# Attention scores of two query tiles made together: second pass on 64 rows, one tile on each row group of TensorE

## The chip, the cores and the metric

The kernel runs on one core of one Trainium2 chip. The metric is the device time of one execution in microseconds (us). Three executions of the kernel before took 3033.25 us in the median, 3031.68 to 3037.04. A profiled execution gives the views that are quoted here; PE is TensorE, PEld its weight loads, DVE is VectorE, ACT ScalarE, POOL GpSimd, SP the engine that issues most transfers.

## What is computed

One layer of a streaming encoder for 2048 prompt frames and 8 x 16 sample frames, all in float32: a mixer (chunked attention beside a convolution module), cross-attention into 256 memory tokens and a gated feed-forward. The change touches the attention of the prompt frames. A query chunk of 64 frames sees its own chunk and the 8 before it, with a bias by relative distance, in 8 heads of 64 channels:

```python
def one_chunk(c):
    start = c * CHUNK
    qc = lax.dynamic_slice_in_dim(q, start, CHUNK, axis=1)
    kc = lax.dynamic_slice_in_dim(k_ext, start, BAND, axis=1)
    ...
    s = jnp.einsum("bqhd,bkhd->bhqk", qc, kc, preferred_element_type=jnp.float32) * scale + bias
    s = jnp.where(valid[None, None, None, :], s, NEG_INF)
    p = jax.nn.softmax(s, axis=-1)
    return jnp.einsum("bhqk,bkhd->bqhd", p.astype(vc.dtype), vc)
```

## The kernel before

The stages follow each other: memory keys and values (to about 150 us), the input projection with the convolution (to 640 us), attention (640 to 925 us), output projection and cross-attention (to about 1600 us), then the feed-forward. Nearly all matmuls take their operands as fp32r, a rounded float32, so each float32 number is split into a high part (`hi`) and a rest (`lo`), and a product is made of two or three matmuls that add up in PSUM.

In the projection, `qk` makes q and k for one pair of heads (`j`) and one group of 384 tokens (`x`), splits them and stores them to DRAM in `self.qs[j]` and `self.ks[j]`, shape [2, 128, 2048]: plane 0 is hi, plane 1 is lo, then 128 channels (two heads of 64), then tokens. The split lands in a buffer `qk`, of which there are two (`qkx` in the last group of tokens), and L717 stores it in one transfer on SP's queue. `qk` runs 24 times for q: 20 times with 384 tokens, 4 times with 128 (tile 15 and the sample frames, whose q is kept on the chip).

In attention, `units` runs over 8 heads and, in each, 16 tiles of 128 queries. `head_load` brings a head in, while the head before is worked on: `q2` holds hi in partitions 0 to 63 and lo in 64 to 127; `k2` holds k's hi twice, in both halves; `kl` holds k's lo twice. `scores` (L850) makes a tile's scores against up to 5 blocks of 128 keys. A matmul with `q2` as weights and `k2` as moving operand contracts over 128 rows and gives (q_hi + q_lo) k_hi; a second one with `kl` adds (q_hi + q_lo) k_lo. With five blocks the keys are cut into 384 and 256 columns, so that each part stays in a PSUM bank; tiles 0 to 3 have 128, 256, 384 and 512 columns. The scores of a tile have a place of 4 KB in PSUM (`"s"`), of which there are two. `softmax_band` adds the bias and finds the maximum on DVE (L793) and takes the exponential on ACT (L795). Four units later `transp` turns the probabilities (L878, transposes of float32 on TensorE, split by ACT at L879 and DVE at L880), six later, at every fourth, `values` multiplies them with v (L891). `sample` does the attention of one sample stream a head between these.

The order on each engine is set by the scheduler of the language, from priorities (the place in the code, raised by `high_priority`), waits and a timeline of its own; `issue_after(ins)` only keeps the block's instructions behind `ins` on its engine. TensorE takes its instructions strictly in that order. Weight loads are instructions of their own, one for each matmul.

Elsewhere TensorE already has matmuls on fewer than 128 rows: L1010 in the output projection (16 rows), L845 in `sample` (16 rows) and, in the feed-forward's `tform`, transposes of 64 rows (L1408).

Of the kernel before, what the change touches and what calls it, by code (L numbers as in the profile page):

```python
# [17 lines left out]
P = 128  # L18
# [5 lines left out]
DH = 64  # L24
# [112 lines left out]
class Build:  # L137
# [309 lines left out]
    def phase_proj(self):  # L447
# [129 lines left out]
        for gi, subs in enumerate(GROUPS):  # L577
# [103 lines left out]
            def qk(which, j, blk, x):  # L681
# [14 lines left out]
                else:  # L696
# [4 lines left out]
                    for i, t in enumerate(sub):  # L701
# [12 lines left out]
                            nc.sync.dma_start(A["new_att_k_sample"][:, PAST - DEC_S:, :], kos[t][:, :])  # L714
                        else:
                            nc.sync.dma_start(A["new_att_k_prompt"][(t - 12) * P:(t - 11) * P, :], kos[t][:, :])
                nc.sync.dma_start(dst[:, :, col:col + npc].rearrange("c p n -> p c n"),  # L717
                                  sp[:, :, :npc].bitcast(F32))

            for j in range(3):  # L720
                for which in (1, 0):
# [61 lines left out]
    def attention(self):  # L783
# [6 lines left out]
        def softmax_band(ps, w, bias, sm):  # L790
            z = self.t(pool, [P, W5], F32, "z", 6)
            nmx = self.t(pool, [P, 1], F32, "nmx", 12)
            nc.vector.tensor_tensor_reduce(out=z[:, :w], in0=ps, in1=bias, scale=-1.0, scalar=3e38,  # L793
                                           op0=ALU.add, op1=ALU.min, accum_out=nmx[:, :])
            nc.scalar.activation(z[:, :w], z[:, :w], AF.Exp, bias=nmx[:, :], scale=-1.0, accum_out=sm)  # L795
            return z
# [50 lines left out]
            nc.vector.tensor_copy(self.attS[:DH, :, ss], po[:DH, :, :DEC_S])  # L847
            nc.vector.tensor_copy(self.attS[DH:, :, ss], po[DH:, :, DEC_S:])

        def scores(hd, t, sm):  # L850
            q2, k2, kl, v2, bt = hd
            j0 = max(0, t - 4)
            nb = t - j0 + 1
            n = nb * P
            tq = slice(t * P, (t + 1) * P)
            ps = self.t(ps_s, [P, 8, P], F32, "s")
            a = 1 if nb == 5 else 0
            for lo, hi in ([(1, 4), (4, 6)] if nb == 5 else [(0, nb)]):
                kk = slice((j0 + lo - a) * P, (j0 + hi - a) * P)
                for x, kx in enumerate((k2, kl)):  # L860
                    nc.tensor.matmul(ps[:, lo:hi, :], q2[:, tq], kx[:, kk], start=x == 0, stop=x == 1)
            return softmax_band(ps[:, a:a + nb, :].rearrange("p a b -> p (a b)"), n, bt[:, W5 - n:], sm)

        def transp(zs, t, quad):
            if t % 4 == 0:
# [50 lines left out]
        for i in range(n + LV + 1):  # L916
            if i < n:
                h, t = units[i]
                if t == 0:
                    fill = sample(h)  # L920
                if t == 6 and h + 1 < H:
                    heads[h + 1] = self.head_tiles(h + 1)
                    self.head_load(h + 1, heads[h + 1], 0, NPT)
                zq[h, t] = scores(heads[h], t, self.sums[:, t, h:h + 1])
            u = i - LT
            if 0 <= u < n:
                h, t = units[u]
# [774 lines left out]
```

## Time and profile before

| | us |
|---|---|
| median of 3 runs | 3033.25 |
| the profiled execution | 3033.59 |
| its span, first to last instruction | 3031.8 |
| TensorE busy in the span | 2949.8 (97%) |
| score matmuls (L861), 448 of them, first and last start | 643.2 to 923.2 |
| granted TensorE clock, mean | 0.987 |

A matmul's row gives its duration from its start to the end of its way through the array; matmuls follow each other faster than that. "Busy" counts the time in which at least one instruction of an engine runs, by these durations. "idle before" and the lists of waits name what ended an engine's idle time. The change acts in two places: the scores (640 to 925 us) and the stores of q (242 to 657 us).

### The profile page before, as it was taken

The numbers are of one execution on the slowest core, as the hardware profiler recorded it, in microseconds if no ns is written. First come the engines' busy times: TensorE is split into PE (matmuls) and PEld (weight loads), VectorE is DVE, ScalarE is ACT, GpSimd is POOL, SyncE is SP. The second block draws the span as 40 slices with busy tenths as digits, with TensorE's granted clock in tenths as the row PEclk, the third lists the DMA queues.
The fourth block names the chain that finished last, engine by engine and source line by source line (L and its number), as shares of the span: only waits on it lengthen the run. The fifth ranks groups of instructions, "written<-read, shape, count | busy, mean of one in ns | idle before, by whom it ended". The sixth has DMA issues, their size and how long they took to land.

```text
span 3031.8 us, 45992 instructions
## 1 busy us (share of the span) xinstructions
PE 2949.8 (97%) x16924; PEld 2715.4 (90%) x16924; DVE 2138.1 (71%) x3077; ACT 1357.7 (45%) x2718; POOL 1397.0 (46%) x1304
## 2 busy tenths in 40 slices
PE   8999999979999999999999999999999999999998
PEld 8999999969997888787888999999999999888786
DVE  6696895957775466535357887888788998656655
ACT  4545454757784345323234333433334444433433
POOL 0267495710012234325356655555555776424413
PEclk9999999989999999999999999999999999999999
DMA  8635255557753556324246433544334446756654
GB/s 300 245 110 188 87 161 163 169 142 182 170 145 134 176 183 227 125 66 144 78 167 216 138 133 119 180 161 160 139 130 153 145 139 208 255 172 208 222 196 163
DMA packets 196429, 500.08 MB, mean 165 GB/s; under 512 B 18981, under 2 KB 82989, under 8 KB 187875
## 3 DMA queue, kind: packets, MB, share of 16 engines
q1 hardware_dynamic: 185883, 461.09, 47.3%
q0 software_dynamic: 10320, 36.05, 3.1%
q8 instruction: 133, 2.18, 0.3%
q14 instruction: 93, 0.76, 0.1%
HBM read 365.97 MB, written 141.81 MB: 167 GB/s over the span
## 4 chain that ended last, share of the span: by engine, by line
PE 40%; DMA 3%; DVE 3%; POOL 2%; issue 1%; ACT 1%; SPq 0%; DVEq 0%; POOLq 0%; ACTq 0%
PE psb L285 13%; PE psb L284 13%; PE psb L283 13%; DMA sbf<-in_w_down_dram 1%; PE psb L291 1%; DMA sbf<-x 1%; POOL sbf L1553 1%; DVE sbr L1614 1%; PE psb L1408 1%; DMA sbf<-hn 0%; DVE sbr L1431 0%; POOL sbf L340 0%; DMA hn<-sbf 0%; DVE flexb L1493 0%; DMA sbf<-in_w_gate_dram 0%
## 5 line engine op out<-in xcount | busy, mean ns | idle before, releaser
L283 PE MATMUL psb<-sbr 128*128 128x384 f32 (+3 forms) x2808 | 943.3, 337 | 4.4 <-ACT sbr L1613 1.4
L284 PE MATMUL psb<-sbr 128*128 128x384 f32 (+3 forms) x2356 | 806.8, 343 | 2.7 <-DVE sbr L320 2.4
L285 PE MATMUL psb<-sbr 128*128 128x512 f32 (+3 forms) x1848 | 633.2, 344 | 3.5 <-DVE sbr L1614 3.4
L283 PEld LDWEIGHTS psb<-sbr 128*128 128x128 f32 x2808 | 531.2, 189 | 34.4 <-ACT sbr L1613 2.8
L285 PE MATMUL psb<-sbr,sbx 128*128 128x384 f32 (+2 forms) x1484 | 477.8, 323 | 0.0
L284 PEld LDWEIGHTS psb<-sbr 128*128 128x128 f32 x2356 | 445.8, 189 | 29.8 <-DVE sbr L320 2.7
L285 PEld LDWEIGHTS psb<-sbr 128*128 128x128 f32 x1848 | 348.1, 189 | 33.3 <-DVE sbr L1614 6.6
L291 PE MATMUL psb<-sbr 128*128 128x512 f32 x1200 | 296.1, 395 | 6.4 <-DVE sbr L1019 1.7
L1431 DVE TENSOR_TENSOR sbr<-sbf,sbr 128x512 fp32r<-128x512 f32 x258 | 263.1, 1023 | 39.7 <-ACT sbr L1430 38.8
L1430 ACT CAST sbr<-sbf 128x512 fp32r<-128x512 f32 x258 | 159.3, 620 | 276.9 <-PE psb L284 231.0
L285 PEld LDWEIGHTS psb<-sbr,sbx 128*128 128x128 f32 x1484 | 281.5, 190 | 0.2
L291 PEld LDWEIGHTS psb<-sbr 128*128 128x128 f32 x1200 | 222.8, 189 | 52.9 <-DVE sbr L1019 1.9
L523 DVE SCALAR_TENSOR_TENSOR psb<-sbf,psb 128x768 f32<-128x768 f32 (+1 forms) x290 | 264.3, 911 | 6.2
L1614 DVE TENSOR_TENSOR sbr<-sbf,sbr 128x384 fp32r<-128x384 f32 (+1 forms) x231 | 170.8, 762 | 94.0 <-ACT sbr L1613 92.1
L278 POOL TENSOR_TENSOR sbx<-sbf,sbr 128x1024 fp32r<-128x1024 f32 x60 | 151.6, 2529 | 80.7 <-ACT sbr L277 77.2
L1613 ACT CAST sbr<-sbf 128x384 fp32r<-128x384 f32 (+1 forms) x231 | 111.0, 497 | 168.3 <-PE psb L284 153.7
L1553 POOL TENSOR_TENSOR sbf<-sbf 128x512 f32<-128x512 f32 x77 | 108.0, 1407 | 167.9 <-DMA sbf<-in_w_down_dram 166.1
L533 POOL TENSOR_TENSOR flexb<-flexb,flexb 128x128 f32<-128x128 f32 (+1 forms) x180 | 169.4, 941 | 22.3 <-ACT flexb L532 12.8
L283 PE MATMUL psb<-sbr,sbx 128*128 128x384 f32 (+1 forms) x524 | 170.6, 327 | 1.6 <-ACT sbx L1430 0.9
L1430 ACT CAST sbx<-sbf 128x512 fp32r<-128x512 f32 x153 | 94.7, 621 | 162.4 <-PE psb L284 150.6
L1431 DVE TENSOR_TENSOR sbx<-sbf,sbx 128x512 fp32r<-128x512 f32 x153 | 152.3, 997 | 15.9 <-ACT sbx L1430 15.5
L277 ACT CAST sbr<-sbf 128x1024 fp32r<-128x1024 f32 x98 | 102.7, 1051 | 107.2 <-PE psb L284 57.6
(336 smaller groups left out, 6246.9 us busy)
## 6 DMA issues: line engine op xcount, KB each, us to landing
af<-flexb SPq DMA_DIRECT2D x33, 1344.0 KB, 6.0
sbf<-in_w_down_dram SPq DMA_DIRECT2D x154, 256.0 KB, 3.8
sbf<-af SPq DMA_DIRECT2D x90, 384.0 KB, 3.9
sbf<-in_w_gate_dram SPq DMA_DIRECT2D x66, 512.0 KB, 3.4
sbf<-in_w_up_dram SPq DMA_DIRECT2D x66, 512.0 KB, 3.4
sbf<-x SPq DMA_DIRECT2D x49, 512.0 KB, 3.9
sbf<-in_w_in_dram SPq DMA_DIRECT2D x48, 512.0 KB, 4.1
sbr<-ks SPq DMA_DIRECT2D x28, 512.0 KB, 10.2
```

The lines of the kernel that those rows point to most:

```text
L278: self.lo_engine.tensor_tensor(lo[:, :], wf[:, :], hi[:, :].bitcast(F32), ALU.subtract)
L283: nc.tensor.matmul(ps, lh, rh, start=start, stop=False, **kw)
L284: nc.tensor.matmul(ps, lh, rl, start=False, stop=False, **kw)
L285: nc.tensor.matmul(ps, ll, rh, start=False, stop=stop, **kw)
L291: nc.tensor.matmul(y[o], l, r[:, o * 512:(o + 1) * 512], start=start and x == 0, stop=stop and x == 2)
L523: nc.vector.scalar_tensor_tensor(acc if w < CW - 1 else o, src(w), cwt[:, j, w:w + 1], acc, ALU.mult, ALU.add)
L533: nc.gpsimd.tensor_tensor(o, o, v, ALU.add)
L1430: nc.scalar.copy(hs[j][:, :], src[j])
L1431: nc.vector.tensor_tensor(ls[j][:, :], src[j], hs[j][:, :].bitcast(F32), ALU.subtract)
L1553: nc.gpsimd.tensor_tensor(acc[:, :], acc[:, :], q[:, :], ALU.add if s > 0 else ALU.subtract)
L1613: nc.scalar.copy(ch[:, m], a[:, x, m])
L1614: nc.vector.tensor_tensor(cl[:, m], a[:, x, m], ch[:, m].bitcast(F32), ALU.subtract)
```

## The change

`scores` now makes two tiles, `t0` and `t0 + 1`, at once. The first pass of both stays as it was, on 128 rows. The second pass multiplies only q_hi with k_lo, on 64 rows (the product q_lo k_lo is left out): the even tile on partitions 0 to 63, the odd tile on 64 to 127, so that the two use different row groups of TensorE. For that, q_hi of an odd tile must lie in the upper half of `q2`: the store of q writes odd tiles with their planes exchanged. The second pass of both tiles is recorded behind the last matmul of the first pass (`issue_after(full.ins)`), with a raised priority, in the order even, odd, even, odd. The count of score matmuls stays at 448: 224 on 128 rows and 224 on 64.

```diff
-                nc.sync.dma_start(dst[:, :, col:col + npc].rearrange("c p n -> p c n"),
-                                  sp[:, :, :npc].bitcast(F32))
+                out = dst[:, :, col:col + npc].rearrange("c p n -> p c n")
+                if which == 1:
+                    nc.sync.dma_start(out, sp[:, :, :npc].bitcast(F32))
+                    return
+                out, src = [x.rearrange("p c (i n) -> p c i n", n=P) for x in (out, sp[:, :, :npc].bitcast(F32))]
+                for odd in range(2):
+                    ii = slice((odd - sub[0]) % 2, npc // P, 2)
+                    if ii.start >= ii.stop:
+                        continue
+                    for c in range(2):
+                        nc.sync.dma_start(out[:, c ^ odd, ii, :], src[:, c, ii, :])
...
-        def scores(hd, t, sm):
+        def scores(hd, t0, sms):
             q2, k2, kl, v2, bt = hd
-            j0 = max(0, t - 4)
-            nb = t - j0 + 1
-            n = nb * P
-            tq = slice(t * P, (t + 1) * P)
-            ps = self.t(ps_s, [P, 8, P], F32, "s")
-            a = 1 if nb == 5 else 0
-            for lo, hi in ([(1, 4), (4, 6)] if nb == 5 else [(0, nb)]):
-                kk = slice((j0 + lo - a) * P, (j0 + hi - a) * P)
-                for x, kx in enumerate((k2, kl)):
-                    nc.tensor.matmul(ps[:, lo:hi, :], q2[:, tq], kx[:, kk], start=x == 0, stop=x == 1)
-            return softmax_band(ps[:, a:a + nb, :].rearrange("p a b -> p (a b)"), n, bt[:, W5 - n:], sm)
+            todo, small = [], []
+            for t in (t0, t0 + 1):
+                j0 = max(0, t - 4)
+                nb = t - j0 + 1
+                tq = slice(t * P, (t + 1) * P)
+                ps = self.t(ps_s, [P, 8, P], F32, "s")
+                a = 1 if nb == 5 else 0
+                rr = slice(t % 2 * DH, (t % 2 + 1) * DH)
+                for x, (lo, hi) in enumerate([(1, 4), (4, 6)] if nb == 5 else [(0, nb)]):
+                    kk = slice((j0 + lo - a) * P, (j0 + hi - a) * P)
+                    full = nc.tensor.matmul(ps[:, lo:hi, :], q2[:, tq], k2[:, kk], start=True, stop=False)
+                    small.append((x, t, ps[:, lo:hi, :], q2[rr, tq], kl[rr, kk]))
+                todo.append((ps[:, a:a + nb, :].rearrange("p a b -> p (a b)"), nb * P))
+            with self.tc.issue_after(full.ins), self.tc.high_priority(offset=HP2):
+                for _, _, out, lhs, rhs in sorted(small, key=lambda v: v[:2]):
+                    nc.tensor.matmul(out, lhs, rhs, start=False, stop=True)
+            return [softmax_band(ps, n, bt[:, W5 - n:], sm) for (ps, n), sm in zip(todo, sms)]
...
-                zq[h, t] = scores(heads[h], t, self.sums[:, t, h:h + 1])
+                if t % 2 == 0:
+                    zq[h, t], zq[h, t + 1] = scores(heads[h], t, [self.sums[:, x, h:h + 1] for x in (t, t + 1)])
```

In the changed kernel L871 is the first pass and L876 the second (both were L861), the transposes are L893 (were L878), the values L906 (were L891), the exponential L804 (was L795), the maximum L802 (was L793), the stores of q L727 (were L717).

The scheduler orders the two kernels differently in attention and, by a row or two, around the stores of q and at the start of the output projection; behind its first tiles no engine's order changes. Three places follow; rows are line, operation, output from inputs, shape of the output and count. The names `sbr` and `sbx` are the SBUF of split operands, `sbf` and `flexb` other SBUF, `psb` is PSUM.

Place 1, TensorE, in head 1. Before, two tiles with five blocks each (tiles 10 and 7), each part of the keys with its two passes:

```order
L812 MATMUL psb<-ident_73,sbf 128x128 x4
L861 MATMUL psb<-sbr 128x384 x2
L861 MATMUL psb<-sbr 128x256 x2
L861 MATMUL psb<-sbr 128x384 x2
L861 MATMUL psb<-sbr 128x256 x2
L878 MATMUL psb<-ident_73,flexb_153 128x128 x8
```

and after, tiles 10 and 11:

```order
L893 MATMUL psb<-ident_73,flexb_153 128x128 x9
L871 MATMUL psb<-sbr 128x384
L871 MATMUL psb<-sbr 128x256
L871 MATMUL psb<-sbr 128x384
L871 MATMUL psb<-sbr 128x256
L876 MATMUL psb<-sbr 128x384 x2
L876 MATMUL psb<-sbr 128x256 x2
L906 MATMUL psb<-sbr 128x128 x2
```

Here the pair stands as the code reads: four matmuls on 128 rows, then four on 64 rows, even, odd, even, odd. A row of 64-row matmuls between two of 128 rows is called a run in what follows; this one has four members.

Place 2, TensorE, a little earlier in head 1. Before, tile 8 and a part of tile 5:

```order
L861 MATMUL psb<-sbr 128x384 x2
L861 MATMUL psb<-sbr 128x256 x2
L812 MATMUL psb<-ident_73,sbf 128x128 x4
L891 MATMUL psb<-sbr 128x512 x2
L861 MATMUL psb<-sbr 128x384 x2
L878 MATMUL psb<-ident_73,flexb_157 128x128 x2
```

and after, the 384 columns of tiles 4 and 5:

```order
L893 MATMUL psb<-ident_73,flexb_153 128x128 x4
L871 MATMUL psb<-sbr 128x384
L876 MATMUL psb<-sbr 128x384
L906 MATMUL psb<-sbr 128x128 x2
L906 MATMUL psb<-sbr 128x256 x2
L906 MATMUL psb<-sbr 128x384 x2
L871 MATMUL psb<-sbr 128x384
L876 MATMUL psb<-sbr 128x384
L906 MATMUL psb<-sbr 128x512
```

Here the pair fell apart: its 256-column part had gone ahead (and with it the matmul that `issue_after` names), and each 384-column part follows alone, so that a run has one member. Over the whole program the 224 matmuls on 64 rows stand in 111 runs: 20 in head 0 and 13 in each of the heads 1 to 7. Of these 13, four have four members, three have two (128 with 256 columns, 256 with 256, 384 with 512), and six have one.

Place 3, ACT, at the start of attention (head 0), where the last q of the projection (L691, tile 15) stands among the first exponentials. Before:

```order
L795 ACTIVATE flexb_153,sbf<-flexb_153,flexb_157 128x128
L795 ACTIVATE flexb_157,sbf<-flexb_157 128x512
L795 ACTIVATE flexb_157,sbf<-flexb_157 128x384
L795 ACTIVATE flexb_153,sbf<-flexb_153,flexb_157 128x640
L879 CAST sbx<-psb 128x512
L553 ACTIVATE flexb_153<-psb,sbf 128x128 x4
L879 CAST sbx<-psb 128x128
L795 ACTIVATE flexb_153,sbf<-flexb_153,flexb_157 128x640
L691 ACTIVATE sbf<-psb 128x128
```

and after:

```order
L804 ACTIVATE flexb_153,sbf<-flexb_153,flexb_157 128x128
L691 ACTIVATE sbf<-psb 128x128
L804 ACTIVATE flexb_157,sbf<-flexb_157 128x512
L804 ACTIVATE flexb_157,sbf<-flexb_157 128x384
L804 ACTIVATE flexb_153,sbf<-flexb_153,flexb_157 128x640
L894 CAST sbx<-psb 128x512
```

L691 moved ahead of four exponentials. It writes a `qkx` buffer whose last content must have been stored, now by four transfers.

## The prediction

> **What bounds the kernel now.** I read the page's first part, then the stretch of the attention in a table by windows, then the waits of the score line in that stretch, and last single matmuls in order of time. The page's row of busy times, and two windows (columns: stretch, its length, then busy us and instructions of PE, PEld, DVE, ACT, POOL, then the granted TensorE clock, DMA share, GB/s):
>
> ```profile
> PE 2949.8 (97%) x16924; PEld 2715.4 (90%) x16924; DVE 2138.1 (71%) x3077; ACT 1357.7 (45%) x2718; POOL 1397.0 (46%) x1304
> ...
> 150.00:640.00 490.00, 481.53 (x3193) 477.29 (x3192) 387.21 (x509) 251.69 (x505) 327.14 (x300) 0.98 0.45 142
> 640.00:680.00 40.00, 28.07 (x158) 23.41 (x156) 21.38 (x57) 22.85 (x65) 3.54 (x7) 0.87 0.79 210
> 680.00:925.00 245.00, 243.30 (x1629) 227.82 (x1626) 188.13 (x451) 194.39 (x446) 20.95 (x30) 0.94 0.61 157
> 925.00:960.00 35.00, 28.48 (x135) 22.65 (x136) 23.15 (x34) 14.22 (x27) 6.02 (x7) 0.94 0.47 155
> ```
>
> The first window is most of the projection; attention runs from 640 to 925 us. In its first 40 us, head 0, TensorE is busy for 28.07 us and so idle for 11.9. In the other 245 us, heads 1 to 7, it is busy for 243.30, and no other engine is over 80%. A nanosecond that the change adds to TensorE there is a nanosecond of the kernel, and so is one it takes away. The score line in that second stretch, and what TensorE's queue waited for before it (us, times):
>
> ```profile
> L861 PE MATMUL psb<-sbr x400: 220/334/795, 680.0 to 923.2; 128*128 128x256 f32 x63, 128*128 128x384 f32 x62, 128*128 128x128 f32 x5, 128*128 128x512 f32 x4
> ...
>   DVE flexb L793: 1.2, 4
> ```
>
> 400 score matmuls (the shapes of a part are listed), and 1.2 us of waiting in all. What one costs is read from start to start, not from its duration, which holds the way through the array. In order of time (start, us, engine, line), 384, 256 and 512 columns:
>
> ```profile
> 2268.29 0.33 PE L285 MATMUL psb<-sbr,sbx 128*128 128x384 f32 x1
> 2268.46 0.33 PE L283 MATMUL psb<-sbr,sbx 128*128 128x384 f32 x1
> ...
> 59.85 0.28 PE L283 MATMUL psb<-sbr 128*128 128x256 f32 x1
> 59.97 0.28 PE L284 MATMUL psb<-sbr 128*128 128x256 f32 x1
> ...
> 994.93 0.84 PE L291 MATMUL psb<-sbr 128*128 128x512 f32 x3
> ```
>
> 0.17 us for 384 columns, 0.12 for 256, and (0.84 - 0.39) / 2 = 0.23 for 512 (one lasts 0.39, in the row at 995.61 below). A tile with five blocks of keys now takes 0.17 + 0.12 twice, 0.58 us.
>
> **A change of the rows in use.** The second pass would run on 64 rows between matmuls on 128. The trace has such places: four transposes on 64 rows in the feed-forward stage, and four matmuls on 16 rows in the output projection. PE and PEld (weight loads) in order of time:
>
> ```profile
> 2268.64 0.34 PE L284 MATMUL psb<-sbr,sbx 128*128 128x384 f32 x1
> 2268.91 0.46 PE L1408 MATMUL psb<-ident,sbf 64*128 64x64 f32 x4
> 2269.30 0.44 PE L285 MATMUL psb<-sbr,sbx 128*128 128x384 f32 x1
> 2269.58 0.34 PE L283 MATMUL psb<-sbr,sbx 128*128 128x384 f32 x1
> ...
> 2268.90 0.33 PEld L1408 LDWEIGHTS psb<-ident,sbf 64*128 64x128 f32 x4 [0.25 <-issue]
> 2269.30 0.19 PEld L285 LDWEIGHTS psb<-sbr,sbx 128*128 128x128 f32 x1
> 2269.41 0.19 PEld L283 LDWEIGHTS psb<-sbr,sbx 128*128 128x128 f32 x1
> ...
> 2269.93 0.14 PEld L1408 LDWEIGHTS psb<-ident,sbf 128*128 128x128 f32 x1
> ...
> 995.61 0.39 PE L291 MATMUL psb<-sbr,sbx 128*128 128x512 f32 x1
> 995.92 0.66 PE L1010 MATMUL psb<-sbr 16*128 16x128 f32 x4
> 996.51 0.96 PE L291 MATMUL psb<-sbr,sbx 128*128 128x512 f32 x3
> ...
> 995.92 0.52 PEld L1010 LDWEIGHTS psb<-sbr 16*128 16x128 f32 x4 [0.35 <-issue]
> ```
>
> First place: from L284 to L283 are 0.94 us. L284 and L285 take 0.17 each, the four transposes 0.06 each ((0.33 - 0.14) / 3 between their loads), together 0.59; 0.35 us are left for the way to 64 rows and back. Second place: from L291 at 995.61 to the third one behind, at 996.51 + 0.96 - 0.39 = 997.08, are 1.47 us; three L291 take 0.68 and four L1010 0.44 (loads (0.52 - 0.19) / 3 = 0.11 apart); again 0.35. The rows also say what it is made of: L284's stream of 0.17 is over at 2268.81, the next load starts at 2268.90, so about 0.10 us pass until the array is empty, and then a load runs that nothing covers, 0.11 us (2269.30 to 2269.41) for this kind of weights. Normally it is under the stream before. For wide score matmuls that makes 2 x (0.10 + 0.11) = 0.42 a round trip, for the measured blocks 0.35; I take 0.40, as the score matmuls load the weights of L1010 and stream longer than L285's load.
>
> **The change, part by part.** (1) *Round trips.* The order shows that the pair doesn't stay together as the code reads: each head from 1 to 7 has 13 runs of 64-row matmuls between 128-row ones, 91 in all: 4 of four matmuls (384 and 256 columns on both row groups), 3 of two (128 with 256, 256 with 256, 384 with 512) and 6 of a single matmul, which overlaps with nothing. 91 x 0.40 = 36.4 us added.
>
> (2) *What overlap gives back.* No row of this trace has two row groups at work, so this is bounded. Nothing overlaps: 0. Both groups load and stream side by side: a run of four takes 0.17 + 0.12 in place of 0.58, saving 0.29; the runs of two save the narrower one's 0.11 (a load's time), 0.12 and 0.17; 28 x 0.29 + 7 x 0.40 = 10.9 us. Between them: streams overlap, loads follow each other 0.11 apart as in the L1010 row: 3 x 0.11 + 0.12 = 0.45, saving 0.13 in a run of four, 0.06 in (384, 512) and nothing in the others, whose streams are no longer than a load: 28 x 0.13 + 7 x 0.06 = 4.1 us. I take 4.1, since every load of the trace, on 16 rows too, keeps that distance.
>
> The Trainium skill, in "TensorE: Matmul & The Clock Gate", Part 3 (what overlaps and what doesn't), says that a load runs beside matmuls in flight if its row group differs, and gives 3.07 times the speed for four row groups at 512 columns; by that the sum is that of the second rival below.
>
> (3) *Head 0* has 20 runs, 15 of them single: 20 x 0.40 = 8.0 us of TensorE in a stretch with 11.9 us of idle time. Between all hidden and none I take half, 4.0.
>
> (4) *The q stores.* 20 stores become four each, 4 become two: 64 more on SP's queue, in pieces of 512 bytes a row instead of 1536. Issue times (ns min/median/max), and the two places in head 0 where a q store is waited for, with the landing:
>
> ```profile
> L717 SPq DMA_DIRECT2D qs<-flexb x16: 359/368/587, 241.9 to 476.3; - x16
> L717 SPq DMA_DIRECT2D qs<-sbf x8: 360/414/674, 583.7 to 657.3; - x8
> ...
> qs<-sbf SPq DMA_DIRECT2D x1, 384.0 KB, 11.5
> ...
> 645.95 0.40 ACT L795 ACTIVATE flexb<-flexb,flexb 128x128 f32<-128x128 f32 x1
> ...
> 656.66 0.28 ACT L691 ACTIVATE sbf<-psb 128x128 fp32r<-128x128 f32 x1 [3.34 <-DMA qs<-sbf]
> ...
> PE psb L812 <- ACT sbf L813: 5.1, 1, 5.1
> ```
>
> 64 x 0.37 to 0.41 = 24 to 26 us of SP's queue, spread over 242 to 657 us. That is 6% of the queue's time there, and TensorE is busy for 481.53 of 490 us of the projection, so the weight loads that stand behind the stores have come in time; nothing is counted for them, with one doubt. ACT's L691 waits 3.34 us for a store that took 11.5 us to land behind head 1's loads, and L813 behind it on ACT keeps TensorE waiting for 5.1. Now four stores must land, up to 3 x 0.41 = 1.2 us later, and L691 stands ahead of four of head 0's exponentials, right behind the one at 645.95: what ACT did from 646.3 to 653.3 then waits too, 7 us at worst. On the other hand fewer loads stand ahead of the stores in SP's order, and the 3.3 us may go. I take 0, ends -3.3 and +8.
>
> (5) *PSUM.* A pair needs both "s" places, so the even tile's first pass waits until DVE has reduced the pair before:
>
> ```profile
> L793 DVE CUSTOM_DVE_ANT_0 flexb<-psb,flexb x136: 274/814/826, 643.8 to 927.7; 128x640 f32<-128x640 f32 x96, 128x256 f32<-128x256 f32 x8, 128x128 f32<-128x128 f32 x8, 128x512 f32<-128x512 f32 x8
> ...
> 808.60 1.03 PE L878 MATMUL psb<-ident,flexb 128*128 128x128 f32 x8
> ```
>
> 0.8 us a tile. Ahead of a pair stand some 9 transposes (place 1 of the order), 8 of which take 1.03 us now, so the first tile's reduction is covered and the second one's partly; what queues behind such a wait on PE is the next transposes, which ACT and DVE wait for. 0, up to 28 x 0.2 = 6.
>
> Sum: 36.4 - 4.1 + 4.0 = 36.3 us onto the profiled execution's 3033.6 (3031.8 of span and 1.8 around it; 0.3 over the median of 3033.25): 3070 us, 1.2% slower. Behind the first tiles of the output projection no queue's order changes, so the delay stays. At the seam (925 to 960 us, TensorE idle for 6.5) loads and splits of its weights move by a row or two on SP and POOL: 0, give or take 3.
>
> **Rivals.** *Faster: fp32r matmuls change from 128 to 64 rows without a drain*, in every run of a head. Then only point (2) is left, 4.1 to 10.9 us saved: with loads side by side 3023. It decides once a round trip costs under 10.9 / 91 = 0.12 us. For it: the 64-row rows are transposes and the fp32r row has 16 rows, so 64 rows and fp32r never met. Against: both show the same 0.35.
>
> *Loads of both groups side by side*: 36.4 - 10.9 + 4.0 = 29.5, that is 3063. For it: the groups share no row of the array. Against: the even 0.11 of all loads.
>
> *No overlap at all*: 36.4 + 4.0, 3074, if the array takes one matmul at a time whatever its rows.
>
> *A change of row group drains as well*: 3 more half trips in 28 runs and 1 in 21, each 0.20: 105 x 0.20 = 21 us, with nothing overlapped 3095. The Trainium skill, in "TensorEngine Tiling (Array Packing)", Key Properties, speaks against it: a change of mode drains, a change of tile alone doesn't; no run here shows it.
>
> *TensorE isn't the bound*, and the drains fill time in which it would have waited for DVE: 3034, the change without effect. Against: 243.30 busy of 245, where PE's queue waited 1.2 us at the scores.
>
> **How the numbers follow.** Forecast 0.42, loads side by side 0.30, no overlap 0.11, drain between groups 0.05, no drain 0.05, hidden 0.03, and 0.04 for something unseen. The first three are one case, slower by 18 to 53 us once the unknowns are in: lowest with the trip at 0.35 (-4.6), side by side, head 0 hidden and the wait gone: 3033.6 + 31.8 - 10.9 - 3.3 = 3051; highest with no overlap, head 0 in full and two thirds of the ends of (4) and (5): 3033.6 + 36.4 + 8 + 9 = 3087. About 0.2% (6 us) is what a measurement of this kernel tells from no change. Faster 0.04 (no drain with a good overlap), same 0.05 (hidden, or no drain with a poor one), slower 0.91.
>
> **What would show it.** The output projection begins with L1010, as the attention ends:
>
> ```profile
> L1010 PE MATMUL psb<-sbr x64: 267/271/323, 932.0 to 1178.7; 16*128 16x128 f32 x64
> ```
>
> From its first to the end of the span about 2100 us should lie as before (932.0 to 3031.8). The stretch from head 1's first score to the last value matmul grows by about 32 us, with PE's idle time before L876's and the following loads growing from about nothing. At each L876 run the load starts 0.27 us or so after the last 384-column start, and the next 128-row matmul's first two loads stand 0.11 apart; in runs of four, L876 starts are 0.11 apart (forecast), nearly equal (side by side) or 0.17 and more (no overlap). I am wrong if L876 loads are prefetched under 128-row streams, or if the attention's waits on DVE L793 (L802 after) make up the growth.

## The result and the profile after

The changed kernel takes 3067.54 us in the median (3065.05 to 3070.22), the kernel before 3032.47 beside it: a ratio of 1.0115, 95% interval 1.0099 to 1.0131, so 35 us or 1.2% slower. The profiled execution has a span of 3068.3 us. Below, differences in us are (ratio - 1) x 3032.5; an interval is some 4 us to either side.

TensorE's share of the span, and the attention by windows (columns as in the prediction; 680 to 925 us holds less of the attention than before, since the last score now starts at 951):

```profile
PE 2997.0 (98%) x16924; PEld 2722.5 (89%) x16924; DVE 2125.2 (69%) x3077; ACT 1356.9 (44%) x2718; POOL 1392.3 (45%) x1304
...
640.00:680.00 40.00, 37.31 (x163) 27.00 (x161) 22.03 (x57) 24.03 (x65) 3.45 (x7) 0.79 0.80 210
680.00:925.00 245.00, 243.82 (x1408) 198.98 (x1407) 162.33 (x388) 165.05 (x382) 11.31 (x25) 0.89 0.58 145
```

TensorE is as full as before (243.82 of 245 us) and does less in it: 1408 matmuls in place of 1629. It had no new waits for other engines to lose that time in; it worked more slowly. The attention as a whole, from its first score to its last value matmul, before and after:

```profile
643.20:945.90 302.70, 288.32 (x1871) 265.42 (x1871) 220.85 (x522) 222.09 (x515) 27.19 (x39) 0.94 0.62 160
643.10:982.60 339.50, 335.04 (x1867) 270.66 (x1867) 219.68 (x521) 223.44 (x515) 27.07 (x39) 0.88 0.55 143
```

With the same number of matmuls but for four, it takes 36.8 us longer. TensorE's idle time in it falls from 14.4 to 4.5 us, and its busy time grows by 46.7. One sign of why is the granted clock, from 0.94 to 0.88. The other is in the weight loads, and not in their busy time (0.14 us a load in both kernels): PEld now stands idle before the loads of the 64-row matmuls.

The waits of the 64-row line's loads, then the list of TensorE's waits over heads 1 to 7 (us, times, longest):

```profile
L876 PEld LDWEIGHTS psb<-sbr x224: 182/183/335, 643.4 to 951.1; 64*128 64x128 f32 x112
its engine sat idle before it (us, times) until:
  issue: 21.3, 97
...
PE psb L871 <- DVE flexb L802: 1.3, 2, 0.9
PE psb L906 <- DVE sbf L912: 1.0, 1, 1.0
```

"issue" is time in which the engine waited for nothing that the profile shows: 0.22 us before each of 97 loads, where the load of a 128-row matmul goes ahead under the stream before it. The drain shows here. Single matmuls at full clock, PE and then PEld in order of time:

```profile
829.25 0.45 PE L871 MATMUL psb<-sbr 128*128 128x384 f32 x1
829.62 0.44 PE L876 MATMUL psb<-sbr 64*128 64x384 f32 x1
829.99 0.39 PE L871 MATMUL psb<-sbr 128*128 128x256 f32 x1
...
829.62 0.18 PEld L876 LDWEIGHTS psb<-sbr 64*128 64x128 f32 x1 [0.19 <-issue]
829.99 0.19 PEld L871 LDWEIGHTS psb<-sbr 128*128 128x128 f32 x1 [0.18 <-issue]
```

Two matmuls of 384 columns take 0.37 us each from start to start, where the stream alone is 0.17: 0.20 on the way to 64 rows and 0.20 on the way back. And a run of four:

```profile
817.42 0.54 PE L871 MATMUL psb<-sbr 128*128 128x384 f32 x2
817.89 0.56 PE L876 MATMUL psb<-sbr 64*128 64x384 f32 x4
818.38 0.66 PE L893 MATMUL psb<-ident,flexb 128*128 128x128 f32 x4
...
817.89 0.30 PEld L876 LDWEIGHTS psb<-sbr 64*128 64x128 f32 x4 [0.19 <-issue]
```

Four matmuls of 64 rows stand between 817.89 and 818.38, 0.49 us with the drain behind them; four loads fit into 0.30 us, where four loads of 16 rows took 0.52 (L1010 before). The trace has the loads of the two row groups, and their matmuls, at most 7 ns apart: they go side by side.

### The profile page after: what moved, and what is told of

It is laid out like the page before. It is cut to its first block, busy times and chain, and to the rows that moved or that the text cites. A ratio compares the mean times of both kernels' runs of the same rounds, so it can differ in the third digit from the quotient of the medians.

```text
span 3068.3 us, 46081 instructions
## 1 busy us (share of the span) xinstructions
PE 2997.0 (98%) x16924; PEld 2722.5 (89%) x16924; DVE 2125.2 (69%) x3077; ACT 1356.9 (44%) x2718; POOL 1392.3 (45%) x1304
## 5 line engine op out<-in xcount | busy, mean ns | idle before, releaser
L1630 DVE TENSOR_TENSOR sbr<-sbf,sbr 128x384 fp32r<-128x384 f32 (+1 forms) x231 | 163.9, 733 | 91.6 <-ACT sbr L1629 88.8
L277 ACT CAST sbr<-sbf 128x1024 fp32r<-128x1024 f32 x98 | 102.5, 1050 | 104.9 <-PE psb L284 55.7
```

The lines of the kernel that those rows point to most:

```text
L1630: nc.vector.tensor_tensor(cl[:, m], a[:, x, m], ch[:, m].bitcast(F32), ALU.subtract)
```

## The experiments

Thirteen measurements with the changed kernel; ratios are to the kernel before, with 95% intervals.

| kernel | median us | ratio | us |
|---|---|---|---|
| changed kernel | 3067.54 | 1.0115 (1.0099 to 1.0131) | +35 |
| stores alone | 3032.30 | 1.0001 (0.9989 to 1.0012) | 0 |
| pairs on 128 rows | 3044.45 | 1.0042 (1.0029 to 1.0056) | +13 |
| lower row group only | 3091.00 | 1.0192 (1.0174 to 1.0209) | +58 |
| 64 rows in tiles 4 to 15 | 3054.31 | 1.0079 (1.0061 to 1.0096) | +24 |
| 32 single runs, tiles 8 to 11 | 3042.02 | 1.0037 (1.0025 to 1.0049) | +11 |
| 32 single runs, tiles 0 to 3 | 3043.45 | 1.0033 (1.0022 to 1.0045) | +10 |
| 96 single runs | 3069.73 | 1.0117 (1.0097 to 1.0136) | +35 |
| pairs kept together | 3049.33 | 1.0053 (1.0037 to 1.0069) | +16 |
| changed kernel, sample on 128 rows | 3043.49 | 1.0039 (1.0025 to 1.0053) | +12 |
| kernel before, sample on 128 rows | 3014.88 | 0.9951 (0.9937 to 0.9964) | -15 |
| the same, output projection too | 3012.52 | 0.9934 (0.9920 to 0.9947) | -20 |
| pairs on 128 rows, sample too | 3028.58 | 0.9996 (0.9987 to 1.0004) | -1 |

**Stores alone.** The changed kernel's stores of q with the scores of the kernel before.

> The stores of q as in the changed kernel (64 transfers more on SP's queue, planes of odd tiles exchanged), the scores as before: tile by tile, both passes on 128 rows, where the exchanged planes give the same sum. Theory (the growth of 35 us comes from TensorE's changes between 128 and 64 rows and from the clock at the head starts): no change, 3030 to 3034 us. Rival (the stores delay head 0 and the projection): up to 3040 us.

Measured: no change, 1.0001. The 64 further transfers cost nothing that shows: from the first score to the last value, the attention takes 299.2 us in this trace and 302.7 in that of the kernel before.

**Pairs on 128 rows.**

```diff
-                    small.append((x, t, ps[:, lo:hi, :], q2[rr, tq], kl[rr, kk]))
+                    small.append((x, t, ps[:, lo:hi, :], q2[:, tq], kl[:, kk]))
```

> The changed kernel with the second pass on all 128 rows (weights q2[:, tq], moving kl[:, kk]): the pairs, the order of the matmuls and the stores stay, the change of rows goes. Theory (row changes): no change from before, 3030 to 3036 us, and TensorE at half clock for about 27 us in heads 1 to 7 as before (65 us in the changed kernel). Rival (the pairs need both places of PSUM, and the new order makes waits on DVE): 3045 us or more, as slow as half of the change or all of it.

Measured: 13 us slower without any change of rows. My theory fell here: part of the loss belongs to the order that the pairs bring. The rival had the right sign and, at 3044.5, nearly its size. The PSUM part of its mechanism isn't borne out: the waits for the maximum (L871 for L802) are 4.7 us from 640 to 985 us, against 5.5 before. The longest waits are for DVE all the same, 7.6 us at L906 for L912, 5.9 of them in head 0. More on such waits comes with the last kernel.

**Lower row group only.** The order on TensorE is nearly the same, with the same count of runs, 111.

```diff
-                        nc.sync.dma_start(out[:, c ^ odd, ii, :], src[:, c, ii, :])
+                        nc.sync.dma_start(out[:, c, ii, :], src[:, c, ii, :])
...
-                rr = slice(t % 2 * DH, (t % 2 + 1) * DH)
+                rr = slice(0, DH)
```

> The changed kernel with all 64-row passes on the lower row group (q's planes not exchanged, rows 0 to 63 for odd tiles too): as many 64-row runs, 111, but nothing in them can go side by side. Theory (the two row groups load and stream side by side, as the starts 2 to 3 ns apart in the changed kernel's trace show): slower than the changed kernel by the narrower stream of every two, 29 runs of four x 0.286 + 21 of two x 0.11 to 0.21 = about 12 us, 3079 us. Rival (the matmuls of the two groups are recorded at the same time, but the array takes them one after the other): the same as the changed kernel, 3067 us.

Measured: 3091, that is 23 us over the changed kernel. Its run of four that answers to the one shown above:

```profile
827.43 0.54 PE L871 MATMUL psb<-sbr 128*128 128x384 f32 x2
827.89 0.85 PE L876 MATMUL psb<-sbr 64*128 64x384 f32 x4
828.68 0.55 PE L893 MATMUL psb<-ident,flexb 128*128 128x128 f32 x3
...
827.89 0.65 PEld L876 LDWEIGHTS psb<-sbr 64*128 64x128 f32 x4 [0.19 <-issue]
```

0.79 us in place of 0.49: the overlap in a run of four is worth 0.30 us, as the two streams that go under make 0.29. So the overlap is real, and the rival falls. The 23 us (give or take 7) are more than the 12 that the rows explain. The half clock goes the same way: the mean granted clock of this kernel's executions is 0.977, that of the changed kernel's 0.981. That is some 24 us more at half clock and, at the 0.3 us each that come out below, 7 us.

**64 rows in tiles 4 to 15 only.**

```diff
-                rr = slice(t % 2 * DH, (t % 2 + 1) * DH)
+                rr = slice(t % 2 * DH, (t % 2 + 1) * DH) if t >= 4 else slice(0, P)
```

> The changed kernel with the second pass on 64 rows in tiles 4 to 15 of each head only; tiles 0 to 3, which stand with the sample at the head starts, have it on 128 rows. The order on TensorE is the changed kernel's. 70 of the 91 runs in heads 1 to 7 remain; by the gaps in the changed kernel's trace they cost 18.7 us over 128 rows, and head 0's some 3. Theory (beside the row changes the clock costs: they keep TensorE at half clock for 65 us in heads 1 to 7 in place of 27, which takes about 9 us): the half clock falls back to about 27 us, and the time is 3055 us. Rival (the clock costs nothing of its own, only the count of runs does, at about the same price each): 3061 us or more, with the half clock where it was.

Measured: 3054.3, the number of the theory, by a sum that was wrong, since it left out the pairs' order: with that at +13 by itself, the runs in tiles 4 to 15 add 11 us and those of tiles 0 to 3 another 11. The half clock did fall back. The profiled execution is no witness for it, at 3065.55 us, 11 over the median; but every execution has its mean granted clock. The clock is either full or half (no other value stands in these traces), so (1 - clock) x 2 x time is an execution's time at half clock, good to some 3 us in the mean of several: 80 us before, 118 in the changed kernel, 90 with the pairs on 128 rows and 91 here. So in the pairs' order it is the runs in tiles 0 to 3, next to the sample, that bring more half clock (27 us); those in tiles 4 to 15 bring none. They are few: 77 of the 91 runs in heads 1 to 7 remain in this trace, not 70.

**Single runs in the order of the kernel before.** Three kernels; tile by tile, the second pass on rows 0 to 63 where the condition holds (`8 <= t < 12 and lo == 1`, `t < 4`, or `t >= 4 and lo == 1`).

```diff
                 for x, kx in enumerate((k2, kl)):
-                    nc.tensor.matmul(ps[:, lo:hi, :], q2[:, tq], kx[:, kk], start=x == 0, stop=x == 1)
+                    rr = slice(0, DH if x and 8 <= t < 12 and lo == 1 else P)
+                    nc.tensor.matmul(ps[:, lo:hi, :], q2[rr, tq], kx[rr, kk], start=x == 0, stop=x == 1)
```

> The kernel before, its order and its stores, with one thing changed: in tiles 8 to 11 of each head the second pass over the 384 columns runs on 64 rows (rows 0 to 63, q_hi with k_lo, the product q_lo k_lo left out there). 32 runs of 64-row matmuls, each of one, four in each head, far from the sample at the head's start. Theory (a change of rows costs a fixed time, 0.30 to 0.40 us for the way there and back, on a TensorE that is the bound): 32 x 0.30 to 0.40 = 10 to 13 us, 3041 to 3045 us; half clock as before, about 27 us in heads 1 to 7. Rival (the pairs' order, not the row change, makes the growth): 3032 us.

Measured: 11.2 us, 0.35 a run (0.24 to 0.46 by the interval).

> As the kernel with 32 runs in tiles 8 to 11, but the 32 runs of one are in tiles 0 to 3 of each head (the whole second pass of these tiles), which stand next to the sample's small matmuls. A few matmuls stand elsewhere in TensorE's order. Theory with the clock (row changes beside the sample's small matmuls leave the array too idle, and the clock stays at half for longer): 10 to 13 us as for the other 32, and some 6 to 9 us more from some 15 to 25 us more at half clock: 3048 to 3053 us. Rival (the clock costs nothing of its own): 3041 to 3045 us or a little less, since head 0 hides a part.

Measured: 10 us, the rival's number. But its condition, a clock that costs nothing, isn't met: the half clock grew as the theory had it, from 78 us to 97 in the mean of whole executions (23 and 12 of them; the one trace has 7 more between 680 and 1000 us). In the trace a run here costs 0.32 us at full clock. The runs and the clock, at 0.3 us for each us at half clock, would make some 16 us together. What takes 6 of them back, no run shows.

> The kernel before with the second pass over the 384 columns on 64 rows in all tiles 4 to 15: 96 runs of one in place of 32. Theory (a fixed price for each run): three times what the 32 runs in tiles 8 to 11 cost, 30 to 39 us, 3062 to 3070 us. Rival (the first runs are hidden in waits that are there anyway, later ones aren't, or the other way round): a price per run that differs from that of the 32 by over a third.

Measured: 35 us, 0.37 a run (0.31 to 0.43). The price is fixed within these intervals: three times the runs, three times the loss. Here too the half clock grew, from 34 to 59 us between 680 and 1000 us, and from 78 to 106 in the mean of whole executions. That takes some 8 of the 35 us and leaves 0.28 a run; the 32 runs in tiles 8 to 11 came with 4 us more, which leaves them 0.31.

**Pairs kept together.**

```diff
-                    full = nc.tensor.matmul(ps[:, lo:hi, :], q2[:, tq], k2[:, kk], start=True, stop=False)
+                    with self.tc.issue_after(full.ins) if full else nullcontext():
+                        full = nc.tensor.matmul(ps[:, lo:hi, :], q2[:, tq], k2[:, kk], start=True, stop=False)
...
-            with self.tc.issue_after(full.ins), self.tc.high_priority(offset=HP2):
-                for _, _, out, lhs, rhs in sorted(small, key=lambda v: v[:2]):
-                    nc.tensor.matmul(out, lhs, rhs, start=False, stop=True)
+            for _, _, out, lhs, rhs in sorted(small, key=lambda v: v[:2]):
+                with self.tc.issue_after(full.ins), self.tc.high_priority(offset=HP2):
+                    full = nc.tensor.matmul(out, lhs, rhs, start=False, stop=True)
```

> The changed kernel with the pair really kept together: each matmul of a pair is recorded behind the one before it (all four first passes, then all four second passes), so that the 224 matmuls on 64 rows stand in 64 runs, 48 of four and 16 of two, in place of 111; none is alone. Theory (each run has a price of 0.30 to 0.40 and gives back the narrower stream of every two, 0.29 in a run of four): 48 x 0.05 + 16 x 0.2 = 6 us for the row changes; the order of pairs by itself costs 13 us, as the pairs on 128 rows measured, and the half clock of the head starts 5 to 8 more: 3050 to 3058 us. Rival (the order of pairs costs because the parts fall apart): 3038 to 3046 us. Rival (no overlap is worth anything): 64 x 0.40 = 26 us and the order's 13: 3070 us.

Measured: 3049.3, just below the theory's range, and 19 us better than the change. Even with 64 runs, 48 of them of four, it is 16 us slower than before: a run of four saves 0.29 and pays some 0.30, and the order costs besides (how much in this order, was not measured by itself).

**The sample on 128 rows.** L854 (L845 before) multiplies 16 rows in four places of each sample. The edit takes away existing row changes, beside the changed kernel and beside the one before:

```diff
-            vn = self.t(pool, [DEC_S, 512], F32, "vn", 2)
-            nc.sync.dma_start(vn[:, :], self.vsamp[s * DEC_S:(s + 1) * DEC_S, :])
+            nc.sync.dma_start(vn[:DEC_S, :], self.vsamp[s * DEC_S:(s + 1) * DEC_S, :])
...
-            pp = self.t(pool, [P, 3, P], F32, "pp", 1)
...
-                nc.tensor.matmul(po[:, c, :], vn[:, cc], pp[:DEC_S, 2, hc], start=False, stop=True)
+                nc.tensor.matmul(po[:, c, :], vn[:, cc], pp[:, 2, hc], start=False, stop=True)
...
+        vn = self.t(pool, [P, 512], F32, "vn", 1)
+        nc.gpsimd.memset(vn[:, :], 0.0)
+        pp = self.t(pool, [P, 3, P], F32, "pp", 1)
+        nc.gpsimd.memset(pp[:, 2, :], 0.0)
```

> The changed kernel with the sample's 16-row matmuls (L854) on 128 rows: the new values and their probabilities lie in tiles of 128 rows that are zeroed once, so that the sum stays the same and four changes of rows in each of the 8 samples go. Order and count of the matmuls stay. In the traces a change there and back costs 0.539 - 3 x 0.110 = 0.21 us. Theory A (these changes, beside the matmuls of 32 columns, are what lets the clock fall at the head starts): 32 x 0.21 = 6.7 us, and the half clock between 680 and 1000 us falls from 72 us to 45 or less, another 8 to 13 us: 3046 to 3053 us. Theory B (the clock falls because matmuls of 32 columns leave the array idle under their loads, whatever their rows): 6.7 us alone, 3061 us.

> The kernel before with the same edit to the sample, the opposite direction of the change: 32 changes of rows fewer. Order as before. Theory A (price of the changes and the clock): 6.7 us and most of the 34 us at half clock between 680 and 1000 us gone, worth 10 or more: 3010 to 3017 us. Theory B (price of the changes alone): 3025 us.

Measured: 23 us (by ratios) off the changed kernel and 15 off the kernel before, theory A in both (the first 2.5 us below its range). The sample in the kernel before, then with the edit:

```profile
682.46 0.53 PE L844 MATMUL psb<-sbf,flexb 128*128 128x32 f32 x4
682.91 0.40 PE L845 MATMUL psb<-sbf 16*128 16x32 f32 x2
683.25 0.63 PE L844 MATMUL psb<-sbf,flexb 128*128 128x32 f32 x4
683.81 0.40 PE L845 MATMUL psb<-sbf 16*128 16x32 f32 x2
684.14 0.63 PE L844 MATMUL psb<-sbf,flexb 128*128 128x32 f32 x4
```

```profile
680.59 0.53 PE L844 MATMUL psb<-sbf,flexb 128*128 128x32 f32 x4
680.96 0.39 PE L845 MATMUL psb<-sbf 128*128 128x32 f32 x2
681.18 0.61 PE L844 MATMUL psb<-sbf,flexb 128*128 128x32 f32 x4
681.63 0.39 PE L845 MATMUL psb<-sbf 128*128 128x32 f32 x2
681.85 0.61 PE L844 MATMUL psb<-sbf,flexb 128*128 128x32 f32 x4
```

One of the four parts takes 0.90 us (683.81 - 682.91) and then 0.67, so 0.23 for each of 32 changes, 7 us in all. The clock is the larger share of the gain. TensorE from 680 to 1000 us in four kernels (before, changed, and each with the edit; the clock is the number behind POOL's count):

```profile
680.00:1000.00 320.00, 311.78 (x1940) 283.03 (x1938) 229.75 (x510) 221.80 (x497) 43.55 (x54) 0.95 0.59 159
```

```profile
680.00:1000.00 320.00, 313.52 (x1769) 255.67 (x1768) 208.50 (x485) 208.94 (x472) 30.02 (x38) 0.89 0.53 139
```

```profile
680.00:1000.00 320.00, 310.76 (x2012) 280.98 (x2011) 234.51 (x516) 223.54 (x503) 48.53 (x60) 0.99 0.61 168
```

```profile
680.00:1000.00 320.00, 310.81 (x1881) 252.89 (x1880) 219.85 (x499) 215.16 (x488) 39.23 (x50) 0.96 0.55 151
```

With a clock that is full or half, 0.89 is (1 - 0.89) x 2 x 320 = 70 us at half clock. The records have 34 us before, 72 after, and 7 and 24 with the edit. 27 us less at half clock gave 15 - 7 = 8 us, 48 us less gave 23 - 7 = 16: about 0.3 us for each. The 66 executions of the kernel before that were measured beside these kernels agree: those with more half clock took longer, by 0.30 us for each us of it (standard error 0.05).

**The output projection's L1010 on 128 rows too**, zeros in 112 rows of `expand` and `rt`:

```diff
-        expand = self.t(pool, [2 * H, 4, 2, DH], F32R, "expand")
+        expand = self.t(pool, [P, 4, 2, DH], F32R, "expand")
+        nc.gpsimd.memset(expand[:, :, :, :].bitcast(F32), 0.0)
...
-        self.rts[t] = self.t(pool, [2 * H, P], F32R, "rt")
-        nc.scalar.copy(self.rts[t][:, :], pt[:2 * H, :P])
+        self.rts[t] = self.rt3[t % 3]
+        nc.scalar.copy(self.rts[t][:2 * H, :], pt[:2 * H, :P])
```

(`rt3` holds three tiles of 128 rows, zeroed once.)

> As the kernel before with the sample on 128 rows, and the output projection's L1010 too: its weights and moving operand have 16 rows of data and 112 of zeros, so that 16 changes of rows go, each of 0.35 us by the rows of the trace before, in a stage where TensorE is the bound. Theory (a fixed price for each change on a bound TensorE): 16 x 0.35 = 5.6 us less than the kernel with the sample alone, 3019 us under theory B of that kernel, and less under theory A. Rival (the zeroing of the rows on GpSimd, or the wider weight loads, give it back): no faster than the kernel with the sample alone.

Measured: 5 us better by the ratios, 2.4 by the medians, with intervals that overlap; it agrees with 16 x 0.35 but does not prove it. This kernel is the fastest of all, 0.9934 of the kernel before.

**Pairs on 128 rows, and the sample too.** The two edits together: an attention without any change of rows.

> The pairs with the second pass on 128 rows, and the sample's L854 on 128 rows too, so that the attention has no change of rows at all and little half clock: what is left between this and the kernel before with the sample on 128 rows (3014.9 us) is the pairs' order alone, and what is left up to the changed kernel with the sample on 128 rows (3043.5 us) is the row changes alone, less the overlap. Theory (the order of pairs costs by waits on DVE and ACT, which row changes partly cover: TensorE's waits from 640 to 985 us are 5 in the list of the changed kernel and 24 in the list of the pairs on 128 rows): 3024 to 3028 us. Rival (the order's 13 us came from the clock): 3015 to 3018 us.

Measured: 14 us above the kernel before with the same edit (0.9996 to 0.9951), half a microsecond above the theory's range: the pairs' order costs 13 to 14 us whether or not the sample lets the clock fall. The attention from its first score to its last value, in the kernel before with the edit and in this one:

```profile
641.20:926.20 285.00, 269.21 (x1871) 249.22 (x1871) 220.67 (x522) 221.00 (x515) 27.18 (x39) 0.99 0.66 170
641.30:939.70 298.40, 275.59 (x1866) 250.75 (x1866) 221.52 (x522) 221.13 (x515) 27.03 (x39) 0.97 0.62 162
```

Of the 13.4 us, idle time of TensorE makes 7.0 (15.8 to 22.8). The half clock in it, 6.8 us and 17.1, makes some 3. TensorE's longest waits in heads 1 to 7 of this kernel, and ACT in order of time at the first:

```profile
PE psb L906 <- DVE sbf L912: 4.3, 1, 4.3
PE psb L893 <- DVE sbr L895: 3.8, 1, 3.8
PE psb L871 <- DVE flexb L802: 1.2, 2, 0.9
```

```profile
863.44 1.04 ACT L277 CAST sbr<-sbf 128x1024 fp32r<-128x1024 f32 x1 [4.89 <-DMA sbf<-in_w_out_dram]
864.51 0.58 ACT L910 COPY flexb<-psb 64x512 f32<-64x512 f32 x1
```

ACT takes L277, the split of the output projection's first weights, before L910, and waits 4.89 us for their transfer; L910, L912 behind it on DVE and TensorE's L906 wait too. The second wait is DVE's: two small instructions on eight numbers a row (L981, L982) that took 0.16 and 0.17 us at 884 us take 1.71 and 2.26 there, ahead of L895. DVE, and POOL at the same time:

```profile
886.02 1.71 DVE L981 CAST sbr<-flexb 128x8 fp32r<-128x8 f32 x1
887.76 2.26 DVE L982 TENSOR_TENSOR sbr<-flexb,sbr 128x8 fp32r<-128x8 f32 x1
889.95 0.68 DVE L895 TENSOR_TENSOR sbr<-psb,sbr 128x512 fp32r<-128x512 f32 x1
...
885.33 2.38 POOL L278 TENSOR_TENSOR sbr<-flexb,sbr 128x1024 fp32r<-128x1024 f32 x1 [5.23 <-DMA sbf<-in_w_out_dram]
887.66 2.33 POOL L278 TENSOR_TENSOR sbr<-sbf,sbr 128x1024 fp32r<-128x1024 f32 x1
```

Each of the two ends within 0.03 us of the end of a POOL instruction that ran when it began (887.73 and 887.71, 890.02 and 889.99). The traces of the fourteen kernels have 45 instructions of this kind and size on DVE that take over 0.3 us: all 45 begin while POOL works and end 21 to 33 ns after one of its instructions, and none that began with POOL at rest is so long. So DVE waits there for POOL's split of the output projection's weights, as far as times alone can show it.

In the kernel before with the same edit no wait in heads 1 to 7 is over 1.0 us. That these places in the order cost is read from the trace of this kernel alone; no kernel with the loads moved was tried. The pairs on 128 rows without the edit lose as much with shorter waits in heads 1 to 7 (1.9 us at most), and their longest, 5.9 us, is in head 0. So what the order costs is shown, and where only in part.

## Why the prediction was right, and where its sum was not

3070 forecast, 3067.5 measured, in the range and on the right side. The mechanism holds: fp32r matmuls do drain between 128 and 64 rows, and each run pays for it on a TensorE that is the bound. But that the number came so close is luck: four terms were off, the overlap, the clock, the order of pairs and the price of a run of four, and they cancelled.

Six of the kernels make a table of their own (us against the kernel before; each difference is good to some 5 us):

| | sample on 16 rows | sample on 128 rows |
|---|---|---|
| order and rows of before | 0 | -14.9 |
| order of pairs, 128 rows | +12.7 | -1.2 |
| order of pairs, 64 rows (the change) | +34.9 | +11.8 |

Down the right column, without the sample's row changes: 13.7 for the order, 13.0 for the row changes. Down the left: 12.7 and 22.2. So the row changes cost 9 us more (give or take 8) where the sample's are there as well. The traces say the same: from the first score to the last value the six take 302.7, 314.5 and 339.5 us down the left, 285.0, 298.4 and 315.7 down the right.

*Round trips, 91 x 0.40.* The count was right. The price was right for single runs on both sides: 0.40 in the rows at 829 us, 0.35 a run in the order of the kernel before, 0.37 with 96 of them. For the runs of four it was too high: from the last 128-row start (817.68 in the single records) to 818.38 are 0.70 us, less 0.12, 0.17 and 0.12 of streams, so some 0.3. What the price is made of was forecast otherwise, as 0.10 us until the array is empty and an uncovered load of 0.11, with the load 0.27 us behind a 384-column start. In the rows it is 0.37 us behind (829.25 and 829.62), and its matmul starts with it: 0.20 us pass before the load.

*Overlap, 4.1 us.* This term was mis-sized, and the choice behind it ("loads follow each other 0.11 apart") is refuted: loads of different row groups go at most 7 ns apart, and an overlap in a run of four is worth 0.30, as the rival "side by side" had it. That rival's 10.9 us would have given 3063. The loads of L1010, on which I rested the choice, are all on the same 16 rows, and no two loads of that trace stood on different row groups: it could not show the case. Nor do all loads keep that distance, as the reason for the choice had it: those of L1408 are 0.06 apart in the prediction's own working. The Trainium skill, "TensorEngine Tiling (Array Packing)", Key Properties, says that tiles can load and multiply in parallel; the trace agrees, with 0.30 us for four loads against 0.65 on one group. The Trainium skill says there too that a change of mode drains and a change of tile does not, and the 0.49 us agree with that too: the rival with drains between groups falls.

Summed run by run in heads 1 to 7 (from the last 128-row start ahead to the first behind, less 0.17, 0.12, 0.23 or 0.11 for each matmul's stream), the 77 runs at full clock added 19.8 us; the 14 at half clock 8.3. The forecast for all 91 was 36.4 less 4.1. Of the 19.8, some 17 belong to the 42 runs of one and about 1 to the 28 runs of four, which save what they cost: the loss by rows is that of the pairs that fell apart.

*The clock, not in the forecast.* It is the step that is missing from the sum. 34 us at half clock became 72, which at 0.3 us each is some 11 us; about 9 of them, by the table, hang on the sample's changes of 16 rows. In the pairs' order nearly all of the growth comes with the runs in tiles 0 to 3, which stand next to the sample (91 us at half clock without them, 118 with them), and 32 single runs in these tiles bring 19 us in the order of the kernel before. But 96 single runs in tiles 4 to 15 bring 28 as well, so the place beside the sample isn't the only condition; what the others have in common is open.

*The order of pairs, 0 to 6.* Priced as waits for PSUM (5) and as "0, give or take 3" at the seam. The PSUM part is right: L871 waited 1.3 us for L802 in heads 1 to 7. The other was wrong as a price of the order by itself, 13 to 14 us. The sentence that "loads and splits of its weights move by a row or two" looked at SP and POOL and passed over what one row of ACT's order does when a transfer is behind it. In the changed kernel little of it is seen as waits (L906 for L912 in heads 1 to 7: 1.0 us, against 4.3). The likely reason, which no run isolates, is that the slower TensorE comes later to the same places; so the terms of the two columns don't add up with the 19.8 us of the rows, which fall partly into those waits.

*Head 0, 4.0.* From its first score to head 1's it grew from 36.8 to 42.2 us, 5.4. That does not bear the term out: the pairs on 128 rows, without any change of rows, take 44.6 us there, and the two orders put different work ahead of head 1's first score. The rows point at a larger price and a larger hidden part: summed as above, head 0's 20 runs add some 11 us (nine ran at half clock), and TensorE's idle time in the whole attention, most of which was in head 0, fell by 9.9. *Stores, 0.* Right.

Of the marks: the stretch from head 1's first score to the last value matmul was to grow by about 32 us and grew by 31.4 (265.9 to 297.3). This agreement says little, since the stretches hold 1731 and 1686 matmuls: in the kernel before, head 1's first score stands ahead of the last ones of head 0. The part behind L1010's first matmul did not stay at 2100 us (956.9 to 3068.3 is 2111.4), because L1026 now starts 25.7 us ahead of the last value matmul, and L1010 started 13.9 ahead; from the last value matmul to the end it did (2085.9 and 2085.7). The waits on L802 stayed small, and no L876 load was prefetched.

## What to carry to other kernels

Where a matmul stream alternates between full rows and a part of them, count the alternations and not the matmuls: here 0.3 to 0.4 us each. A run of four packed matmuls saved 0.30 and so came out even; a run of one only paid. The same count run backwards is a cheap gain: rows of zeros that keep a small matmul in the full-row mode made this kernel 0.5% faster. And when a change reorders an engine by a row, look for a wait on a transfer that now stands ahead of what others need, and at the granted clock, before calling it free.

## What was unexpected of the hardware

The half clock comes in stretches of 3.41 us and its multiples in these traces: 6.83, 10.24 and, in head 0 of the changed kernel, 17.07. The Trainium skill, "TensorE: Matmul & The Clock Gate", Part 1, gives a free-running window of 3.41 us after which an idle array falls to half clock; the stretches agree. What the runs add is how full such an array looks in the other columns. Around one sample of the changed kernel (835.8 to 846.1 us) TensorE is busy all the time and runs at a mean clock of 0.67:

```profile
835.80:846.10 10.30, 10.30 (x55) 9.04 (x54) 5.47 (x16) 5.73 (x15) 0.00 (x0) 0.67 0.95 202
```

"Busy" is no sign of a full clock. A sample has 24 matmuls of 32 columns with four changes of rows (682.46 to 685.93 in the kernel before, 3.5 us). In the kernel before, six of the eight samples are followed by half clock, 3.41 or 6.83 us of it; in the changed kernel all eight are, by 6.83 or 10.24. The same 24 without the changes (680.59 to 683.19, 2.6 us) are followed by none in any of the eight samples of the kernel before with the edit, and by one stretch of 3.41 us in the kernel with the output projection on 128 rows too.
